# Token sums and value-bias sums bound between a tile's maximum and its reciprocal, and the block sum on VectorE, in a Hymba block on one core

## The chip, the cores and the metric

One Trainium2 chip, one of its cores. The metric is the time of one execution on the device in microseconds (us), as the median of several runs. The engines of a core work from instruction queues of their own, each strictly in its own order: TensorE (PE; matmuls, and PEld for its weight loads), VectorE (DVE), ScalarE (ACT), GpSimd (POOL) and SyncE (SP), which issues most of the transfers. Engines wait for one another by semaphores.

## What is computed

One encoder block for 512 tokens of width 2048 in float32: adaLN-modulated norm, one projection of which the columns feed 16 attention heads (64 wide, three dilated windows merged by their softmax denominators) and 4 heads of gated linear attention (GLA), gates on both, an output projection, a residual step and a last norm. Cut to what matters here:

```python
mod = jax.nn.silu(c) @ w_cond[layer] + b_cond[layer]
shift, scale, gate = jnp.split(mod, 3, axis=-1)
h = rms_norm(x) * (1.0 + scale[:, None]) + shift[:, None]
proj = h @ w_in[layer]
aq, ak, av, ag, gq, gk, gv, gg, lr_f, lr_b = jnp.split(proj, PROJ_SPLITS, axis=-1)
...
for window, dilation in DILATED_PATTERNS:
    o_p, lse_p = dilated_window_attention(aq, ak, av, rel_bias, window, dilation)
...
mix_w = jax.nn.softmax(jnp.stack(lses, axis=0), axis=0)
att = jnp.einsum('pbsh,pbshe->bshe', mix_w.astype(av.dtype), jnp.stack(outs, axis=0))
a_out = att.reshape(B, S, ATT_WIDTH) * jax.nn.silu(ag)
...
g_out = g_o * jax.nn.silu(gg)
y = jnp.concatenate([a_out, g_out], axis=-1) @ w_out[layer]
x = x + gate[:, None] * y
return rms_norm(x) * final_gain
```

## The kernel before

**Products.** Each float32 product is made of three matmuls of a reduced type (`three`, L216 to L220): high by high, low by high, high by low. The high part of a weight block (128x1024) is written by ScalarE (`split_hi`, L481), the low part by VectorE as raw minus high (`split_lo`, L466). Tiles are named by unit and block: raw_qk61 is the loaded weight, qk61h and qk61l its parts. The value projection V and the output products O save multiplications by a recursive scheme that needs sums of blocks. Sums over tokens of the normalised input (`token_sums`, from L1115; tiles S1 to S4) are made by VectorE in ten operations of 128x512 for each of four parts and stored for V. Most block sums are made in transfers that add on arrival (`paced`, L418, in GpSimd's queue). The block named T1 of the output products is the exception: two blocks are loaded (raw_O and raw_P, L380), and `whole` (L455) adds them on GpSimd, four times for each of the two pairs of output products: for O16 to O19 and O44 to O47.

**Units.** TensorE's order is the order of the program. `unit(name)` is one pass over the eight weight blocks of a projection, with side work put in at set fractions of it. The units from 190 us on are qk2, qk4, qk6, gk (each with the attention of four heads at its side), V, ag0, ag1, gg0, gg1 (each with one GLA head), and then the products O: pair 0 is O0 to O27, pair 1 is O28 to O55. On the other engines a scheduler sets the order by its estimate of when operands are there; `tc.issue_after(x)` binds one instruction behind another on its engine.

**Attention.** One tile is 128 queries of one head against 512 keys, 16 tiles a unit. VectorE adds the bias row and takes the maximum (L773, out p, st), ScalarE makes the exponential with its sum (L776), VectorE the reciprocal (L777), GpSimd the scaled probabilities p (L781), TensorE transposes p (L793), ScalarE and VectorE split the transposed tile (pt, L797 and L798), and TensorE multiplies it with the values (L807).

**Sums beside.** The shift of the norm passes through the value projection as a bias. It is a product of a row with a matrix, made by VectorE in 16 halves of 128x1024 (`bias_half`; load L882, tile rawv, sums L888 for the first and L317 for the second half of a row block). The gate of the residual step is made in the same way in 32 halves (`gate_half`, load L846, tile rawg, sums L317). Halves of one kind share the four buffers of the raw weights; the others have a pool `two` with a single buffer each for the tags l and h. Before the change the token sums and the bias sums are side work at fractions of a unit, bound behind the last low part (`last["lo"]`). `SUMS_IN` says how many bias and gate sums a unit takes, `SUM_OPS_IN` how many of the block sums by transfer.

**GLA.** In each of ag0 to gg1, `gla_head` computes a chain of states on TensorE (kv, L965) and VectorE (st, L972 and L977), masked copies of the scores (L997), the gated squares (gsq, gsl, L1027) and their sum over rows (gn).

**The last load.** One weight block of the end, O52, is loaded and split ahead of its turn; its high part is called wlast.

## Time and profile before

| | |
|---|---|
| Median of 3 runs | 943.13 us (943.1 to 943.54) |
| Profiled execution, its time | 945.4 us |
| Profiled execution, its span | 943.6 us |
| Mean granted TensorE clock | 0.989 |
| TensorE busy | 912.2 us (97%) |
| VectorE busy | 714.8 us (76%) |
| ScalarE busy | 490.6 us (52%) |
| GpSimd busy | 141.7 us (15%) |

A row of a timeline gives the start and the length in us, the engine, the line in the kernel, the operation, out<-in, the tile's shape, and in brackets the idle time before it and what ended it. A row of the waits gives who waited at which line, for what, and then total, times and longest in us. A row of the windows gives the stretch, the busy time and number of instructions of each engine (PE, PEld, DVE, ACT, POOL), the granted clock, the share of DMA time and GB/s. A row of the groups gives busy time in us and the mean of one in ns, then the idle time before them.

### The profile page before, as it was taken

To read this page: it belongs to the slowest core of one execution; us is meant where nothing else is said; L and a number is where in the kernel's file an instruction comes from. 1 tells how busy PE (TensorE), PEld (TensorE's weight loads), DVE (VectorE), ACT (ScalarE), POOL (GpSimd) and SP (SyncE) were. 2 spreads that over 40 slices of the span, in tenths; PEclk is the share of its full clock that TensorE was granted. 3 is DMA by queue.
4 is the path that set the end of the run, shared out by engine and by line. 5 is a ranking of instruction groups with operands and counts; after the bars stand their busy time and mean duration, and the time that the engine had idled before them with its cause. 6 is when DMAs were issued, how large, how long until landed. Compare 5 with 4: busy or idle time off the path is not lost.

```text
span 943.6 us, 12252 instructions
## 1 busy us (share of the span) xinstructions
PE 912.2 (97%) x4327; PEld 753.3 (80%) x4327; DVE 714.8 (76%) x1028; ACT 490.6 (52%) x790; POOL 141.7 (15%) x176
## 2 busy tenths in 40 slices
PE   8999999999999999999999999999979999999976
PEld 6888888888878788788777888888868888788854
DVE  7988899777777787787578677684957469796676
ACT  5553543555645555555567545453634157455454
POOL 0000000022223242242000112021120100400311
PEclk9999999999999999999999999999989999999989
DMA  9999497676797877986777788787866978878643
GB/s 352 404 412 376 174 371 257 217 200 195 198 266 231 258 215 217 249 234 195 226 255 248 242 250 264 223 257 255 235 194 217 289 225 317 310 237 283 234 171 141
DMA packets 62247, 238.13 MB, mean 252 GB/s; under 512 B 8197, under 2 KB 8485, under 8 KB 52841
## 3 DMA queue, kind: packets, MB, share of 16 engines
q1 hardware_dynamic: 55282, 194.77, 57.8%
q0 software_dynamic: 6464, 42.01, 19.2%
q8 instruction: 34, 0.56, 0.2%
q10 hardware_dynamic: 440, 0.57, 0.2%
q14 instruction: 27, 0.22, 0.1%
HBM read 224.64 MB, written 50.42 MB: 292 GB/s over the span
## 4 chain that ended last, share of the span: by engine, by line
PE 80%; DVE 7%; DMA 6%; ACT 3%; issue 2%; POOL 1%; SPq 0%; ACTq 0%; DVEq 0%; POOLq 0%
PE ps_qk L218 4%; PE ps_qk L220 4%; PE ps_qk L219 4%; PE g L220 3%; PE g L219 3%; PE g L218 3%; PE stb L220 3%; PE stb L218 3%; PE stb L219 3%; PE ps_ag L218 3%; PE ps_ag L220 3%; PE ps_ag L219 3%; PE o L807 3%; PE t L793 3%; PE sta L219 2%
## 5 line engine op out<-in xcount | busy, mean ns | idle before, releaser
L781 POOL TENSOR_SCALAR p<-p,st 128x512 f32<-128x512 f32 x62 | 53.7, 866 | 187.1 <-DVE st L777 164.6
L776 ACT ACTIVATE p<-p,st 128x512 f32<-128x512 f32 x64 | 46.2, 722 | 55.9 <-DVE st L773 53.9
L317 DVE CUSTOM_DVE_ANT_0 cb<-cb,sb,c_bcond 128x2048 f32<-128x2048 f32 (+1 forms) x32 | 73.5, 2296 | 1.1 <-DMA cb<-in_wm 1.1
L773 DVE CUSTOM_DVE_ANT_0 p<-s,g 128x512 f32<-128x512 f32 x64 | 43.8, 687 | 12.7 <-PE s L770 12.2
L798 DVE TENSOR_TENSOR pt<-t,pt 128x512 fp32r<-128x512 f32 x64 | 43.7, 687 | 11.9 <-ACT pt L797 11.6
L418 POOL DMA_DIRECT2D T<-in_w_o x32 | 23.2, 732 | 159.1 <-ACT V2h L481 15.3
L797 ACT ACTIVATE pt<-t 128x512 fp32r<-128x512 f32 x64 | 37.9, 591 | 14.4 <-PE t L793 13.4
L793 PEld LDWEIGHTS t<-c_ident,p 128*128 128x128 f32 x256 | 31.3, 140 | 12.4 <-POOL p L781 4.4
L793 PE MATMUL t<-c_ident,p 128*128 128x128 f32 x256 | 38.6, 273 | 2.4 <-POOL p L781 2.3
L455 POOL TENSOR_TENSOR raw_O<-raw_O,raw_P 128x1024 f32<-128x1024 f32 x8 | 21.1, 2643 | 115.3 <-DMA raw_P<-in_w_o 62.7
L807 PEld LDWEIGHTS o<-pt,vv 128*128 128x128 f32 x256 | 34.8, 188 | 2.8
L807 PE MATMUL o<-pt,vv 128*128 128x256 f32 x256 | 35.6, 281 | 0.0
L769 PE MATMUL s<-ks,qs 128*128 128x512 f32 x64 | 25.1, 392 | 1.2 <-DVE pt L798 1.2
L982 ACT ACTIVATE sq<-st,sc 128x256 f32<-128x256 f32 x24 | 12.1, 505 | 25.6 <-DVE st L972 17.6
L770 PE MATMUL s<-kl,qs 128*128 128x512 f32 x64 | 25.0, 391 | 0.0
L317 DVE CUSTOM_DVE_ANT_0 rawg<-rawg,crow,gate 128x1024 f32<-128x1024 f32 x16 | 20.4, 1280 | 5.6 <-DMA rawg<-in_wg 5.6
L418 POOL DMA_DIRECT2D T3V<-in_w_gv x8 | 5.5, 693 | 119.8 <-ACT qk21h L481 119.8
L777 DVE RECIPROCAL st<-st 128x1 f32<-128x1 f32 x64 | 10.1, 158 | 16.3 <-ACT p L776 16.3
L418 POOL DMA_DIRECT2D T<-T x16 | 9.1, 572 | 80.0 <-ACT V6h L481 13.8
L317 DVE CUSTOM_DVE_ANT_0 rawg<-rawg,crow,c_bcond 128x1024 f32<-128x1024 f32 x16 | 20.3, 1279 | 0.3 <-DMA rawg<-in_wg 0.3
L810 ACT ACTIVATE oh<-o 64x256 f32<-64x256 f32 x32 | 12.2, 382 | 12.2 <-PE o L807 11.8
L545 ACT ACTIVATE h_hi<-xt,shift 128x512 fp32r<-128x512 f32 x16 | 11.5, 718 | 13.0 <-DVE shift L317 13.0
(1640 smaller groups left out, 3081.5 us busy)
## 6 DMA issues: line engine op xcount, KB each, us to landing
cb<-in_wm SPq DMA_DIRECT2D x31, 1024.0 KB, 9.0
T<-in_w_o POOLq DMA_DIRECT2D x32, 512.0 KB, 7.2
rawg<-in_wg SPq DMA_DIRECT2D x32, 512.0 KB, 5.4
raw_O<-in_w_o SPq DMA_DIRECT2D x32, 512.0 KB, 4.3
raw_qk<-in_w_qk SPq DMA_DIRECT2D x24, 512.0 KB, 4.1
raw_O<-T SPq DMA_DIRECT2D x24, 512.0 KB, 5.3
rawb<-in_w_sb SPq DMA_DIRECT2D x16, 512.0 KB, 5.4
rawv<-in_wv SPq DMA_DIRECT2D x16, 512.0 KB, 4.7
```

What stands on the lines that cost most here:

```text
L218: mm(ps, lh, rh, start=first, stop=False, skip_group_check=more)
L219: mm(ps, ll, rh, start=False, stop=False, skip_group_check=more)
L220: mm(ps, lh, rl, start=False, stop=last, skip_group_check=more)
L317: nc.vector.tensor_tensor_reduce(out=w, in0=w, in1=with_, op0=ALU.mult, op1=ALU.add, scale=1.0, scalar=init, accum_out=dst)
L418: move = nc.gpsimd.dma_start(dst, src, max_dma_last_dim=8192, **how).ins
L773: nc.vector.tensor_tensor_reduce(out=t, in0=ps, in1=gt[h][:, P * i:P * i + 512], op0=ALU.add, op1=ALU.min, scale=1.0, scalar=3e38, accum_o ...
L776: act(t, t, AF.Exp, bias=st[:, 0:1], scale=-1.0, accum_out=st[:, 1:2])
L781: last["pool"] = nc.gpsimd.tensor_scalar(t, t, st[:, 2:3], 1.0, op0=ALU.mult, op1=ALU.mult).ins
L793: nc.tensor.transpose(pk[:, kt * P:kt * P + P], t[:, kt * P:kt * P + P], ident)
L797: act(hi, src, AF.Copy)
L798: tt(lo, src, hi.bitcast(F32), op=ALU.subtract)
L807: mm(po[:, :256], vv[h // 4][:, kt, h % 4, :], t[:, w, kt, :], start=kt == 0 and w == 0, stop=kt == 3 and w == 1)
```

## The change

A string for each attention unit, `BESIDE`, says for each of its 16 tiles whether a token operation (t), a bias sum (r) or nothing stands beside it. `beside(top)` binds that operation behind the tile's maximum, and the reciprocal is bound behind the operation. A bias sum's load is issued five tiles ahead (`BIAS_AHEAD`). The bias sums leave `SUMS_IN`; with their names gone from it, the units qk4, qk6 and gk fetch their weights three blocks ahead instead of two (L1060). gg0 takes eight gate sums instead of nine, gg1 eight instead of seven, and each gate sum's load is issued 1.1 instead of 0.8 of a sum's share ahead of the sum's number. `SUM_OPS_IN` spreads the same number of transfers a little differently. `whole` adds its two blocks on VectorE.

```diff
 GLA_AT = (0.01, 0.02, 0.33, 0.46, 0.46, 0.56, 0.64, 0.76, 0.76, 0.88)
 GLA_FIRST = (0.27, 0.32, 0.53, 0.6, 0.74, 0.78, 0.84, 0.89, 0.91, 0.97)
 
-SUMS_IN = {"qk4": 5, "qk6": 5, "gk": 6, "ag0": 8, "ag1": 8, "gg0": 9}
+SUMS_IN = {"ag0": 8, "ag1": 8, "gg0": 8}
+
+BESIDE = {"qk2": " tttt ttt ttt", "qk4": " tttttrttrtrttrr", "qk6": " rttrttrttrttrtt", "gk": "rttrttrttrttrttr"}
+BIAS_AHEAD = 5
 
 
 OUT_ORDER = ("P1", "P7", "P6", "P4", "P5", "P3", "P2")
...
 WEIGHTS = {"P1": "11", "P7": "T3", "P6": "T2", "P4": "T4", "P5": "T1", "P3": "22", "P2": "21"}
 BLOCK_SUMS = {"T3": ("12", "22"), "T2": ("T3", "11"), "T4": ("T2", "21"), "T1": ("11", "12")}
 OUT_DEEP = 6
-SUM_OPS_IN = {"qk2": 10, "qk4": 9, "qk6": 9, "gk": 8, "V": 8, "ag0": 9, "ag1": 9, "gg0": 9, "gg1": 9}
+SUM_OPS_IN = {"qk2": 10, "qk4": 10, "qk6": 10, "gk": 9, "V": 9, "ag0": 8, "ag1": 8, "gg0": 8, "gg1": 8}
 
 
 def _plan(tasks, free, ready):
...
 
     def cond_sum(dst, w, with_, init):
 
-        nc.vector.tensor_tensor_reduce(out=w, in0=w, in1=with_, op0=ALU.mult, op1=ALU.add,
-                                       scale=1.0, scalar=init, accum_out=dst)
+        return nc.vector.tensor_tensor_reduce(out=w, in0=w, in1=with_, op0=ALU.mult, op1=ALU.add,
+                                              scale=1.0, scalar=init, accum_out=dst)
 
     grow = dp.tile([NH, 1024], F32, tag="grow", name="grow")
...
     def whole(i):
         if i in second:
             t, e = raws[i], second.pop(i)
-            nc.gpsimd.tensor_tensor(t, t, e, op=ALU.add)
+            tt(t, t, e, op=ALU.add)
 
     def split(i):
         split_hi(i)
...
 
     cat = [None] * 4
 
+    side_work = []
+
+    def beside(top):
+
+        go = side_work.pop(0) if side_work else None
+        if len(side_work) >= BIAS_AHEAD and side_work[BIAS_AHEAD - 1]:
+            load = side_work[BIAS_AHEAD - 1][0]
+            if load:
+                load()
+        if not go:
+            return None
+        with tc.issue_after(top):
+            return go[1]()
+
     def attention(pairs):
 
         tiles = [(2 * p + j, i) for p in pairs for j in range(2) for i in range(4)]
...
                 mm(ps, qs[:, q], kl, start=False, stop=True)
                 t = T2(f"p{h}{i}")
                 st = sm.tile([P, 3], F32, tag="st", name=f"st{h}{i}", bufs=6)
-                nc.vector.tensor_tensor_reduce(
+                top = nc.vector.tensor_tensor_reduce(
                     out=t, in0=ps, in1=gt[h][:, P * i:P * i + 512], op0=ALU.add, op1=ALU.min,
-                    scale=1.0, scalar=3e38, accum_out=st[:, 0:1])
+                    scale=1.0, scalar=3e38, accum_out=st[:, 0:1]).ins
                 act(t, t, AF.Exp, bias=st[:, 0:1], scale=-1.0, accum_out=st[:, 1:2])
-                nc.vector.reciprocal(st[:, 2:3], st[:, 1:2])
+                held = beside(top)
+                with tc.issue_after(held) if held else nullcontext():
+                    nc.vector.reciprocal(st[:, 2:3], st[:, 1:2])
                 if (h, i) in ((15, 2), (15, 3)):
                     act(t, t, AF.Copy, scale=st[:, 2:3])
                 else:
...
 
         def go():
             raw = t[0]
-            with tc.issue_after(last["lo"]):
-                if z == 0:
-                    nc.vector.tensor_tensor_reduce(out=raw, in0=raw, in1=shb[0][:, :1024], op0=ALU.mult, op1=ALU.add,
-                                                   scale=1.0, scalar=0.0, accum_out=vbias0[:, m:m + 1])
-                else:
-                    cond_sum(vbias[:, m:m + 1], raw, shb[0][:, 1024:], vbias0[:, m:m + 1])
+            if z == 0:
+                return nc.vector.tensor_tensor_reduce(out=raw, in0=raw, in1=shb[0][:, :1024], op0=ALU.mult, op1=ALU.add,
+                                                      scale=1.0, scalar=0.0, accum_out=vbias0[:, m:m + 1]).ins
+            return cond_sum(vbias[:, m:m + 1], raw, shb[0][:, 1024:], vbias0[:, m:m + 1]).ins
         return load, go
 
-    sum_work = [bias_half(m, z) for m in range(8) for z in range(2)]
-    sum_work += [gate_half(m, z) for z in range(2) for m in range(KT)]
+    bias_work = [bias_half(m, z) for m in range(8) for z in range(2)]
+    sum_work = [gate_half(m, z) for z in range(2) for m in range(KT)]
 
     def some_sums(name):
         r = [sum_work.pop(0) for _ in range(SUMS_IN.get(name, len(sum_work)))]
         n = len(r)
-        loads = [(max(q - 0.8, 0.05) / n, x[0]) for q, x in enumerate(r)]
+        loads = [(max(q - 1.1, 0.05) / n, x[0]) for q, x in enumerate(r)]
         return sorted(loads + [((q + 0.7) / n, x[1]) for q, x in enumerate(r)], key=lambda x: x[0])
 
     def gla_head(h):
...
 
         def sub(n, h, th, kh):
             made[n], made[n + "3"] = pair_tile(f"{n}{kp}")
-            tt(made[n + "3"], h_part(h, th, kh, kp), h_part(h, 1, 0, kp), op=ALU.subtract)
+            return tt(made[n + "3"], h_part(h, th, kh, kp), h_part(h, 1, 0, kp), op=ALU.subtract).ins
 
         def low_sub(n, th, kh):
-            sub(n + "e", h_lo, th, kh)
+            return sub(n + "e", h_lo, th, kh)
 
         def whole_sum(n):
-            tt(made[n], made[n], made[n + "e"], op=ALU.add)
+            i = tt(made[n], made[n], made[n + "e"], op=ALU.add).ins
             s_store(n, kp, made[n])
+            return i
 
         def s2():
             made["S2"], made["S23"] = pair_tile(f"S2{kp}")
-            stt(made["S23"], made["S13"], -1.0, h_part(h_hi, 0, 0, kp), op0=ALU.mult, op1=ALU.subtract)
+            return stt(made["S23"], made["S13"], -1.0, h_part(h_hi, 0, 0, kp), op0=ALU.mult, op1=ALU.subtract).ins
 
         def s2_low():
-            tt(made["S23"], made["S23"], h_part(h_lo, 0, 0, kp), op=ALU.subtract)
+            i = tt(made["S23"], made["S23"], h_part(h_lo, 0, 0, kp), op=ALU.subtract).ins
             s_store("S2", kp, made["S2"])
+            return i
 
         def s4():
             made["S4"], made["S43"] = pair_tile(f"S4{kp}")
-            tt(made["S43"], made["S23"], h_part(h_hi, 0, 1, kp), op=ALU.add)
+            return tt(made["S43"], made["S23"], h_part(h_hi, 0, 1, kp), op=ALU.add).ins
 
         def s4_low():
-            tt(made["S43"], made["S43"], h_part(h_lo, 0, 1, kp), op=ALU.add)
+            i = tt(made["S43"], made["S43"], h_part(h_lo, 0, 1, kp), op=ALU.add).ins
             s_store("S4", kp, made["S4"])
+            return i
 
         parts = [lambda: sub("S3", h_hi, 0, 0), lambda: low_sub("S3", 0, 0), lambda: whole_sum("S3"),
                  lambda: sub("S1", h_hi, 1, 1), lambda: low_sub("S1", 1, 1), lambda: whole_sum("S1"),
                  s2, s2_low, s4, s4_low]
 
-        def held(go):
-            def run():
-                with tc.issue_after(last["lo"]):
-                    go()
-            return run
-        return [((q + 0.3) / len(parts), held(go)) for q, go in enumerate(parts)]
+        return parts
 
     cond_row = dp.tile([1, 2048], F32, tag="cond_row", name="cond_row")
     nc.sync.dma_start(cond_row, sb[0:1, :])
...
 
     for p in range(2):
         qk_evict(p, psb["b", 4 + 2 * p], psb["b", 5 + 2 * p])
+    for kp, n in enumerate(("qk2", "qk4", "qk6", "gk")):
+        sums = token_sums(kp)
+        for c in BESIDE[n].ljust(16):
+            side_work.append(None if c == " " else (None, sums.pop(0)) if c == "t" else bias_work.pop(0))
+        assert not sums
+    assert not bias_work
+
     for n, p in (("qk2", 0), ("qk4", 2), ("qk6", 4)):
-        ps = unit(n, False, attention((p, p + 1)) + token_sums(p // 2)
-                  + ([(0.05, shift_row)] if p == 2 else []) + (some_sums(n) if p else []))
+        ps = unit(n, False, attention((p, p + 1)) + ([(0.05, shift_row)] if p == 2 else []))
         for q in range(2):
             qk_evict(p + 2 + q, ps[2 * q], ps[2 * q + 1])
 
-    ps = unit("gk", False, attention((6, 7)) + token_sums(3) + some_sums("gk"))
+    ps = unit("gk", False, attention((6, 7)))
     gla["k"] = B8("gkt", [4, 512])
     for i in range(4):
         act(gla["k"][:, i, :], ps[i], AF.Copy)
```

TensorE's order is the same in both. The rows below give line, operation, out<-in and shape; the changed kernel's lines are 3 to 21 higher. On VectorE, in the middle of unit qk4 (names: p and st of head 7, tile 0 and 1; pt, t the transposed tile; qk60l a low part), before:

```order
L773 ISA p70_2688,st70_2689<-s70_2685,g7_2584 128x512
L773 ISA st70_2689 128x1
L777 RECIPROCAL st70_2689<-st70_2689 128x1
L798 TENSOR_TENSOR pt61_2700<-t62_2701,pt61_2700 128x4x128
L466 TENSOR_TENSOR qk60l_2816<-raw_qk60_2731,qk60h_2815 128x1024
L773 ISA p71_2739,st71_2740<-s71_2736,g7_2584 128x512
L773 ISA st71_2740 128x1
L814 TENSOR_TENSOR cat0_1594<-o60_2716,oh60_2725 64x256
L888 ISA rawv20_2654,vbias0_1495<-rawv20_2654,shb_2263 128x1024
```

and in the changed kernel (head 6, tiles 1 and 2; rawv01 is a bias sum, S21 a token sum):

```order
L790 ISA p61_2590,st61_2591<-s61_2587,g6_2433 128x512
L790 ISA st61_2591 128x1
L320 ISA rawv01_2393,vbias_1494<-rawv01_2393,shb_2259,vbias0_1495 128x1024
L320 ISA vbias_1494 128x1
L796 RECIPROCAL st61_2591<-st61_2591 128x1
L817 TENSOR_TENSOR pt51_2558<-t53_2605,pt51_2558 128x4x128
L790 ISA p62_2618,st62_2619<-s62_2615,g6_2433 128x512
L790 ISA st62_2619 128x1
L1151 TENSOR_TENSOR S21_2542<-S21_2542,h_lo_154 128x512
```

The sums stand between a maximum (ISA p, st) and its reciprocal, one for a tile.

On VectorE in the unit gg0, where the gate sums (rawg) meet the chain of states (st300 and what follows), before:

```order
L317 ISA rawg41_6140,gate_1492<-rawg41_6140,crow1_5771,gate0_1493 128x1024
L317 ISA gate_1492 128x1
L317 ISA rawg51_6197,gate_1492<-rawg51_6197,crow1_5771,gate0_1493 128x1024
L317 ISA gate_1492 128x1
L972 TENSOR_SCALAR st300_6182<-kv300_6177,sc30_6007 128x256
L1336 TENSOR_TENSOR A11l_6431<-cat0_1594,A11h_6430 128x1024
L1336 TENSOR_TENSOR A11l_6431<-cat1_2986,A11h_6430 128x1024
L977 SCALAR_TENSOR_TENSOR st301_6186<-kv300_6177,sc30_6007,dc301_6187 128x256
```

and in the changed kernel:

```order
L989 TENSOR_SCALAR st300_6184<-kv300_6179,sc30_6012 128x256
L1357 TENSOR_TENSOR A11l_6429<-cat1_2984,A11h_6428 128x1024
L994 SCALAR_TENSOR_TENSOR st301_6188<-kv300_6179,sc30_6012,dc301_6189 128x256
L469 TENSOR_TENSOR gg06l_6264<-raw_gg06_6211,gg06h_6263 128x1024
L994 SCALAR_TENSOR_TENSOR st302_6193<-kv301_6180,sc30_6012,dc302_6194 128x256
L989 TENSOR_SCALAR st310_6231<-kv310_6226,sc31_6039 128x256
L994 SCALAR_TENSOR_TENSOR st311_6235<-kv310_6226,sc31_6039,dc311_6236 128x256
L994 SCALAR_TENSOR_TENSOR st312_6240<-kv311_6227,sc31_6039,dc312_6241 128x256
L469 TENSOR_TENSOR gg07l_6312<-raw_gg07_6266,gg07h_6311 128x1024
L1014 COPY_PREDICATED at3_6281<-c_maskf_1486,att30_6271 128x512
L1016 SCALAR_TENSOR_TENSOR at3_6281<-c_ident_1484,at3_6281 128x512
L320 ISA rawg51_6206,gate_1492<-rawg51_6206,crow1_5762,gate0_1493 128x1024
```

The sum of rawg51 has moved from ahead of st300 to behind the whole chain and the masked copy of at3.

On VectorE in pair 1 of the output products, from the low part O40l on (x, y and gx belong to the residual step of the pair before), before:

```order
L466 TENSOR_TENSOR O40l_7608<-raw_O40_7524,O40h_7607 128x1024
L466 TENSOR_TENSOR O41l_7632<-raw_O41_7546,O41h_7631 128x1024
L466 TENSOR_TENSOR O42l_7652<-raw_O42_7570,O42h_7651 128x1024
L466 TENSOR_TENSOR O43l_7672<-raw_O43_7588,O43h_7671 128x1024
L466 TENSOR_TENSOR O44l_7693<-raw_O44_7610,O44h_7692 128x1024
L466 TENSOR_TENSOR O45l_7724<-raw_O45_7634,O45h_7723 128x1024
L1430 TENSOR_TENSOR y23_7711<-gx10_7465,u210_7627 128x512
L1430 TENSOR_TENSOR y33_7717<-gx11_7466,u211_7629 128x512
L1423 TENSOR_TENSOR y23_7711<-y23_7711,gate_b_6749 128x512
L1423 TENSOR_TENSOR y33_7717<-y33_7717,gate_b_6749 128x512
L1424 TENSOR_TENSOR x11_7551<-y23_7711,x11_7551 128x512
L1424 TENSOR_TENSOR x11_7551<-y33_7717,x11_7551 128x512
```

and in the changed kernel:

```order
L469 TENSOR_TENSOR O40l_7608<-raw_O40_7524,O40h_7607 128x1024
L458 TENSOR_TENSOR raw_O44_7610<-raw_O44_7610,raw_P44_7612 128x1024
L469 TENSOR_TENSOR O41l_7632<-raw_O41_7546,O41h_7631 128x1024
L469 TENSOR_TENSOR O42l_7652<-raw_O42_7570,O42h_7651 128x1024
L458 TENSOR_TENSOR raw_O45_7634<-raw_O45_7634,raw_P45_7636 128x1024
L458 TENSOR_TENSOR raw_O46_7654<-raw_O46_7654,raw_P46_7656 128x1024
L469 TENSOR_TENSOR O43l_7672<-raw_O43_7588,O43h_7671 128x1024
L469 TENSOR_TENSOR O44l_7693<-raw_O44_7610,O44h_7692 128x1024
L458 TENSOR_TENSOR raw_O47_7674<-raw_O47_7674,raw_P47_7676 128x1024
L1451 TENSOR_TENSOR y23_7711<-gx10_7465,u210_7627 128x512
L469 TENSOR_TENSOR O45l_7724<-raw_O45_7634,O45h_7723 128x1024
```

The four additions of raw_P, which were the last work in GpSimd's order ahead of the last norm, now stand among the low parts, that of O47 ahead of O45l.

## The prediction

> **What bounds the kernel now.** I read the page first (span and busy shares), then TensorE's waits, then the windows, because a share of 97% says nothing about where the other 3% lie.
>
> ```profile
> span 943.6 us, 12252 instructions
> PE 912.2 (97%) x4327; PEld 753.3 (80%) x4327; DVE 714.8 (76%) x1028; ACT 490.6 (52%) x790; POOL 141.7 (15%) x176
> ...
> PE kv L965 <- DVE st L977: 5.3, 1, 5.3
> PE g L218 <- ACT O47h L481: 2.9, 1, 2.9
> ...
> PE t L793 <- POOL p L781: 2.3, 3, 0.9
> PE g L220 <- DVE O46l L466: 2.0, 1, 2.0
> ...
> PE g L220 <- DVE O18l L466: 1.0, 1, 1.0
> ```
>
> TensorE is the bound. Its instructions stand in the same order in both kernels, so the change can only take away or add time in which TensorE waits, and time at a lowered clock. A wait's columns are total, times, longest. The windows place them (TensorE, weight load, VectorE, ScalarE, GpSimd busy, then the granted clock, the DMA share and GB/s):
>
> ```profile
> 200.00:260.00 60.00, 59.37 (x323) 49.76 (x322) 44.04 (x91) 35.97 (x72) 17.23 (x26) 1.00 0.71 198
> 260.00:330.00 70.00, 67.61 (x357) 56.31 (x356) 53.22 (x110) 37.27 (x72) 19.40 (x25) 1.00 0.85 252
> 330.00:400.00 70.00, 68.87 (x364) 57.52 (x363) 54.67 (x111) 38.93 (x74) 21.53 (x25) 1.00 0.81 228
> ...
> 550.00:680.00 130.00, 130.00 (x639) 109.75 (x638) 95.88 (x131) 68.02 (x109) 18.77 (x31) 1.00 0.80 252
> 690.00:700.00 10.00, 4.69 (x18) 3.55 (x17) 6.04 (x8) 2.91 (x4) 4.21 (x3) 0.87 0.53 179
> 700.00:710.00 10.00, 10.00 (x45) 8.32 (x44) 4.41 (x8) 3.46 (x6) 1.75 (x3) 0.79 0.54 125
> 810.00:830.00 20.00, 19.04 (x84) 15.47 (x83) 18.77 (x18) 10.17 (x16) 6.56 (x3) 1.00 0.94 345
> 890.00:900.00 10.00, 8.43 (x38) 6.64 (x36) 9.37 (x9) 1.80 (x2) 4.91 (x2) 1.00 0.63 214
> 900.00:910.00 10.00, 5.64 (x16) 3.79 (x17) 6.04 (x11) 5.12 (x8) 0.00 (x0) 0.78 0.50 176
> 910.00:920.00 10.00, 10.00 (x41) 8.15 (x40) 8.60 (x11) 7.33 (x13) 1.15 (x1) 0.88 0.48 173
> ```
>
> Four places lose time within reach of the change. **A**, the unit gg0 at 690 to 710: 5.31 us idle, and 10 × 0.13 + 10 × 0.21 = 3.4 us at the lowered clock, 8.7 together. **B**, the second pair of output products at 890 to 920: 1.57 + 4.36 idle and 10 × 0.22 + 10 × 0.12 = 3.4 of clock, 9.3 together. **C**, the first pair: 0.96. **D**, the attention units: 0.63 + 2.39 + 1.13 = 4.15. The clock falls only behind the two long stops; the shorter stops of C and D leave it at 1.00.
>
> The Trainium skill, page "TensorE: Matmul & The Clock Gate", section "What's actually happening", says that the clock halves after an idle window of about 3.4 us; the trace agrees, as the windows around the 5.3 us stop show and those around stops of 1 us do not. By that rule a stop that shrinks from 5.3 to 2 us gives back the clock's 3.4 us too; read from the rows alone, A and B pay the clock together with the stop.
>
> **Part A, the gate sums.** What VectorE did there:
>
> ```profile
> 693.28 1.28 DVE L317 CUSTOM_DVE_ANT_0 rawg<-rawg,crow,gate 128x1024 f32<-128x1024 f32 x1 [5.58 <-DMA rawg<-in_wg]
> ...
> 719.49 0.68 DVE L1027 TENSOR_TENSOR gsl<-gsq,gsh 128x512 fp32r<-128x512 f32 x1
> ```
>
> A gate sum waited 5.58 us for its transfer and stood ahead of the state st300, on which the chain to kv (5.3 us) hangs. gg0 had nine sums; it now has eight, as ag0 and ag1 have, and in the new order this sum stands behind the whole state chain and the masked copies. The nearest rows for that placement are those of ag0 and ag1: 130.00 of 130.00 us busy from 550 to 680. Between no loss (those windows) and the full 8.7 I take 0.3 left, since the placement is the same and the sums' loads are issued 0.3 of a sum earlier. So A gives **−8.4**. What is late next: a sum that waits now holds the splits behind it and, at the end of gg0, the chain to gsl, which ended at 719.49 + 0.68. That is rival 2.
>
> **Part B, the block sums.** Eight sums of two loaded 128x1024 blocks move from GpSimd to VectorE.
>
> ```profile
> 880.24 3.10 POOL L455 TENSOR_TENSOR raw_O<-raw_O,raw_P 128x1024 f32<-128x1024 f32 x1 [61.20 <-DMA raw_P<-in_w_o]
> 886.67 5.73 POOL L455 TENSOR_TENSOR raw_O<-raw_O,raw_P 128x1024 f32<-128x1024 f32 x2 [3.33 <-DVE O43l L466]
> 896.23 2.51 POOL L455 TENSOR_TENSOR raw_O<-raw_O,raw_P 128x1024 f32<-128x1024 f32 x1 [3.82 <-DMA raw_O<-in_w_o]
> ...
> 902.67 1.06 ACT L481 ACTIVATE wlast<-raw_O 128x1024 fp32r<-128x1024 f32 x1 [9.17 <-DMA raw_O<-in_w_o]
> ...
> 904.86 1.04 ACT L481 ACTIVATE O47h<-raw_O 128x1024 fp32r<-128x1024 f32 x1
> ...
> 890.77 2.71 DVE L466 TENSOR_TENSOR O45l<-raw_O,O45h 128x1024 fp32r<-128x1024 f32 x1 [0.63 <-ACT O45h L481]
> ...
> 895.55 0.39 PE L220 MATMUL g<-O45l,c_h 128*128 128x512 f32 x1
> ...
> L1232 DVE TENSOR_TENSOR vS<-rawS,vS 128x1024 fp32r<-128x1024 f32 x8 | 9.7, 1221 | 1.5 <-ACT vS L1231 1.5
> ```
>
> This is one chain: each sum frees the buffer that the next load needs. It holds four sums (3.10 + 5.73 + 2.51 = 11.34) and three gaps with a load (3.33, 3.82, and from 898.74 to 902.67 3.93). ScalarE works in order, so O47h stood behind wlast, which waited 9.17 us for the last of these loads; TensorE's 2.9 us for O47h comes from there. VectorE adds two 128x1024 blocks in 1.22 (the vS row, the same operation and shape with another output type), so four sums take 4.88 and the chain is 6.46 shorter: wlast at 896.2, O47h 2.19 behind it at 898.4, done by 899.4. Without stops TensorE comes to O47 at 895.55 + 22 × 0.227 = 900.5 (0.227 from the starts of successive matmuls, 895.55 and 895.78). So that wait is gone with 1.1 to spare.
>
> What VectorE pays is 4 × 1.22 = 4.9 us in a stretch in which it was 9.37 of 10 busy; but that busy time holds splits that were stretched beside GpSimd's sums (O45l 2.71 instead of about 1.22), so most of it is given back. Queued behind a waiting sum are the splits of the blocks before it: sum47 stands ahead of O45l, which TensorE needs at 895.55. By the chain above sum47 starts at 896.23 − 1.88 − 2 × 1.64 = 891.1 at the earliest (1.88 and 1.64: what the first and each of the next two sums save), O45l ends near 894 to 895. O46l, behind four additions of y and x, comes at about 898.5 against its need at 898.3. I take 1.0 of loss left, between 0 and 3 (one transfer gap). B gives **−8.3**.
>
> The Trainium skill, page "SBUF — State Buffer", section "Who interferes with whom", says that a VectorE instruction with two SBUF inputs and a GpSimd instruction that reads SBUF exclude each other for a whole instruction. The O45l row agrees: 2.71 beside a GpSimd sum. By that rule the splits fall back to the 1.22 used above; the same rule speaks against the attention part, since the bound sums would hold up GpSimd's normalisation of probabilities.
>
> **Part C, the same sums in the first pair.**
>
> ```profile
> 813.36 3.33 DVE L466 TENSOR_TENSOR O17l<-raw_O,O17h 128x1024 fp32r<-128x1024 f32 x1 [0.52 <-ACT O17h L481]
> ...
> 820.71 1.22 DVE L466 TENSOR_TENSOR O18l<-raw_O,O18h 128x1024 fp32r<-128x1024 f32 x1
> ...
> raw_O<-in_w_o SPq DMA_DIRECT2D x32, 512.0 KB, 4.3
> ```
>
> O17l loses its 2.1 us of stretch, but O16l and O17l now stand behind sums 17 to 19, and the load for sum 19 waits for a buffer that an earlier split frees behind sum 17. With 4.3 us for that load O17l ends between 819 and 820 and O18l between 823 and 824; the old stop here was 0.96. The new loss lies between 0 and 3; I take 2, so C costs **+1.0**.
>
> **Part D, the bound sums beside attention.** 40 token operations and 16 bias sums exist before and after; nothing is added, they move to between a tile's maximum and its reciprocal.
>
> ```profile
> 270.48 1.23 DVE L888 CUSTOM_DVE_ANT_0 rawv<-rawv,shb 128x1024 f32<-128x1024 f32 x1 [2.17 <-DMA shb<-srow]
> ...
> 315.57 1.22 DVE L466 TENSOR_TENSOR qk61l<-raw_qk,qk61h 128x1024 fp32r<-128x1024 f32 x1
> 316.71 0.16 DVE L777 RECIPROCAL st<-st 128x1 f32<-128x1 f32 x1
> 316.78 1.27 DVE L317 CUSTOM_DVE_ANT_0 rawv<-rawv,shb,vbias 128x1024 f32<-128x1024 f32 x1
> ...
> 312.61 0.69 POOL L781 TENSOR_SCALAR p<-p,st 128x512 f32<-128x512 f32 x1 [2.09 <-DVE st L777]
> ...
> 317.04 1.57 POOL L781 TENSOR_SCALAR p<-p,st 128x512 f32<-128x512 f32 x1 [3.01 <-DVE st L777]
> ...
> 316.46 0.60 PE L793 MATMUL t<-c_ident,p 128*128 128x128 f32 x4
> ```
>
> Between maximum and reciprocal VectorE waits for ScalarE's exponential anyway, so a bias sum (1.27) sets a reciprocal back by less than its length. For a middle tile that is covered: its p ends at 312.61 + 0.69 = 313.30 and is transposed at 316.46, 3.16 us later. Without this cover each of the 16 would cost up to 1.27. The last tile of a unit has no such cover: there TensorE goes straight from p to the transposes, and the three waits of 2.3 us are of that kind (317.04 + 1.57 = 318.61). At the end of qk4 the reciprocal now stands ahead of qk61l but behind a bias sum of about the same length: no change there. What goes: the wait of the first bias sum for its row (2.17, which made a stop of about 1.3), now ordered seven tiles into qk4; the first tile of qk4, which had two token operations ahead of its maximum and now has one behind it (0.63 in the window 200 to 260); and some of the rest. Of 4.15, 2.1 go: **−2.1**, between 0 and −3.
>
> The weights of qk4, qk6 and gk are fetched three instead of two ahead, and each bias sum holds its buffer for five tiles. At the start of V, the second block's buffer is freed by the last bias sum:
>
> ```profile
> 450.49 0.69 DVE L773 CUSTOM_DVE_ANT_0 p<-s,g 128x512 f32<-128x512 f32 x1 [0.89 <-PE s L770]
> ...
> 462.41 0.39 PE L220 MATMUL ps_gv_P<-V1l,h_hi 128*128 128x512 f32 x1
> ...
> rawv<-in_wv SPq DMA_DIRECT2D x16, 512.0 KB, 4.7
> ```
>
> Last maximum to 451.2, sum to 452.4, load 4.7, splits 1.04 + 1.22: 459.4, needed at 462.41. 3 us of cover that a queue on SP can eat; I take **+0.3**, and **+0.5** for places that I could not follow (GpSimd's queue gives up 8 sums and takes DMA issues in another rhythm).
>
> **Sum:** −8.4 − 8.3 + 1.0 − 2.1 + 0.3 + 0.5 = −17.0. The profiled span of 943.6 becomes 926.6. The run of that profile took 945.4, 2.3 over the median 943.13, so the sum is applied to the median: **926.1**.
>
> **The rivals.** *One: sums that wait for transfers hold the splits behind them.* VectorE works in order, GpSimd had nothing behind its sums. If sum47 and sum19 each wait one transfer gap (3.3 to 3.9) longer than I assume, B keeps a stop of about 3 with its 3.4 of clock and C loses 3: 926.1 + 5.4 + 1 = **932.5**. For it: VectorE already waited 5.58 for a transfer in A. Against: both loads are issued as soon as a buffer is free, and buffers now come free 6.46 sooner.
>
> *Two: the stop of A only moves.* The sums stay bound in VectorE's order; the late one now stands ahead of a split and of the last sums of gg0, and the load after it needs its buffer. If the chain to gsl is 2 to 4 late, a stop of 3 with 3.4 of clock replaces A: 926.1 + 6.1 = **932.2**. For it: gsl needs the end of this very queue. Against: the 130.00 of 130.00 in the two units with eight sums.
>
> *Three, the other side: the bound bias sums wait.* A sum in front of a reciprocal whose transfer is late holds that tile's p, the next pt and the next maximum. It decides once a wait exceeds the cover of 3.16; with 16 sums it takes about 17 / 16 + 3.16 = 4.2 us of wait for each to eat the whole gain. At half of them waiting 6.5, the loss is 8 × 3.3 = 27: **953**. For it: odd halves share one buffer, so a load can wait for an earlier sum. Against: five tiles are 5 × 260 / 64 = 20 us (64 tiles between 200 and 460), and the transfer takes 4.7.
>
> *Four: the binding does nothing.* The sums fall where they fell and D stays: 926.1 + 2.1 = **928.2**. For it: the first maxima's stops may come from the matmuls ahead of them, not from the sums.
>
> **How the numbers follow.** Forecast 0.60, own range 919 to 931 (A from 0 to 2 left, B and C from 0 to 3 each, D from 0 to −3, V from 0 to 2); rival one 0.12; two 0.12; three 0.10; four 0.06. The range 919 to 936 leaves out rival three, a gain beyond 24, and rivals one and two with both losses at once: not quite 2 in 10. This kernel's measurement cannot tell 0.2% (1.9 us) from nothing. Rival three is slower in 0.09 of its 0.10, and 0.01 lies within; one and two together may add 0.01 there; the rest is faster: 0.89.
>
> **What would show it.** A: TensorE busy over 9.8 of 10 in the windows of the old stop, granted clock 1.00, no wait of kv on st over 0.5. B: four VectorE sums of about 1.2 us, wlast before 898, no wait for O47h, clock 1.00 at its place. C: a wait for O17l or O18l of 0 to 3. D: GpSimd's p waiting for st as before, only the waits at the ends of units left. I am wrong if TensorE waits for p in middle tiles, if a clock under 1.00 stays in either place, or if VectorE shows waits on bias transfers above 3 us.

## The result, and the profile after

| | Before | After |
|---|---|---|
| Median on one chip | 943.34 us (943.1 to 944.27, 4 runs) | 928.09 us (926.28 to 931.5, 4 runs) |
| Ratio | | 0.9841, 95% interval 0.9812 to 0.987 |
| Profiled execution: time, span | 945.4, 943.6 us | 931.5, 929.7 us |

The kernel became 15.3 us faster; 17.0 were forecast, and 928.09 stands in the range of 919 to 936. Both profiled executions lie above their medians: the changed kernel's by 3.4 us, as the slowest of its four, and the one before by 2.1.

First TensorE's waits in the changed kernel (its lines are 3 to 21 higher than before), those of 0.5 us and more, without sta and warm at the kernel's start:

```profile
PE ps_gv_P L221 <- DVE gv L1318: 2.2, 1, 2.2
PE g L223 <- DVE O55l L469: 1.9, 1, 1.9
PE t L812 <- POOL p L800: 1.5, 2, 0.8
...
PE g L223 <- DVE O18l L469: 0.8, 1, 0.8
PE g L223 <- DVE O46l L469: 0.5, 1, 0.5
```

The waits of kv (5.3) and of O47h (2.9) are gone. Two rows were not among the prediction's: gv in V, and O55l, the low part of the last block. The windows say what each costs with its clock. First one row of the kernel before that was not shown yet, the unit V:

```profile
460.00:550.00 90.00, 88.59 (x417) 71.00 (x416) 60.70 (x67) 52.20 (x75) 7.19 (x12) 1.00 0.77 244
```

and then the changed kernel:

```profile
200.00:260.00 60.00, 59.98 (x326) 50.50 (x325) 44.16 (x90) 35.12 (x68) 16.65 (x26) 1.00 0.75 199
260.00:330.00 70.00, 68.86 (x364) 57.66 (x363) 53.02 (x109) 38.38 (x73) 18.04 (x26) 1.00 0.88 254
330.00:400.00 70.00, 69.38 (x367) 58.38 (x367) 55.70 (x115) 38.26 (x74) 17.44 (x27) 1.00 0.83 239
...
460.00:550.00 90.00, 87.64 (x409) 71.02 (x408) 57.26 (x62) 49.85 (x71) 6.87 (x12) 0.98 0.78 250
690.00:700.00 10.00, 10.00 (x54) 8.63 (x53) 6.40 (x9) 3.92 (x7) 3.48 (x5) 1.00 0.65 177
700.00:710.00 10.00, 10.00 (x66) 9.03 (x65) 7.33 (x11) 2.89 (x4) 0.78 (x1) 1.00 0.88 243
800.00:820.00 20.00, 19.23 (x85) 15.53 (x84) 18.71 (x22) 10.30 (x16) 0.00 (x0) 1.00 0.88 315
880.00:890.00 10.00, 9.47 (x42) 7.28 (x41) 7.64 (x11) 4.11 (x6) 0.00 (x0) 1.00 0.75 261
890.00:900.00 10.00, 10.00 (x46) 8.21 (x45) 9.96 (x17) 6.81 (x12) 0.00 (x0) 1.00 0.47 159
900.00:910.00 10.00, 9.84 (x44) 7.83 (x42) 9.55 (x13) 7.05 (x13) 2.72 (x2) 1.00 0.56 210
910.00:920.00 10.00, 8.21 (x28) 6.33 (x28) 5.95 (x13) 3.90 (x10) 1.25 (x1) 0.83 0.09 35
```

| Place | Lost before | Lost after | Change | Forecast |
|---|---|---|---|---|
| A, gg0 | 8.7 | 0.0 | −8.7 | −8.4 |
| B, second output pair | 9.3 | 0.5 | −8.8 | −8.3 |
| C, first output pair | 1.0 | 0.8 | −0.2 | +1.0 |
| D, attention | 4.15 | 0.02 + 1.14 + 0.62 = 1.8 | −2.4 | −2.1 |
| V | 1.4 | 2.36 + 90 × 0.02 = 4.2 | +2.8 | +0.3 |
| O55l, at the end | 0 | 0.16 + 1.79 + 10 × 0.17 = 3.7 | +3.7 | 0 |
| Not followed | | | | +0.5 |

The column adds to −13.6, against −13.9 in the spans. In the table, "lost" is idle time plus time at the lowered clock. A second reading needs neither: TensorE's order is the same in both kernels and both traces hold its 4327 matmuls, so the starts of the same matmul can be compared. By them A gives −8.5, B −8.2, C −0.2, D −3.1, V +1.8 and O55l +3.8, −14.4 up to the last matmul (934.06 before, 919.63 after); from there to the end the changed kernel took 0.5 longer. So V cost 1 us less than the table says and D gave 0.7 more; the rest agrees.

VectorE's timeline shows how B was won:

```profile
869.88 1.23 DVE L458 TENSOR_TENSOR raw_O<-raw_O,raw_P 128x1024 f32<-128x1024 f32 x1 [1.56 <-DMA raw_P<-in_w_o]
...
875.55 1.22 DVE L458 TENSOR_TENSOR raw_O<-raw_O,raw_P 128x1024 f32<-128x1024 f32 x1 [1.80 <-DMA raw_O<-in_w_o]
877.00 1.23 DVE L458 TENSOR_TENSOR raw_O<-raw_O,raw_P 128x1024 f32<-128x1024 f32 x1 [0.23 <-DMA raw_P<-in_w_o]
...
882.58 1.23 DVE L458 TENSOR_TENSOR raw_O<-raw_O,raw_P 128x1024 f32<-128x1024 f32 x1 [2.08 <-DMA raw_O<-in_w_o]
...
884.32 1.22 DVE L469 TENSOR_TENSOR O45l<-raw_O,O45h 128x1024 fp32r<-128x1024 f32 x1
```

and ScalarE's what became of wlast:

```profile
887.65 1.06 ACT L484 ACTIVATE wlast<-raw_O 128x1024 fp32r<-128x1024 f32 x1 [4.28 <-DMA raw_O<-in_w_o]
...
889.23 1.04 ACT L484 ACTIVATE O47h<-raw_O 128x1024 fp32r<-128x1024 f32 x1
```

Four sums of 1.23 us in place of 11.34 in all, O45l at 1.22 instead of 2.71, and wlast waits 4.28 instead of 9.17. From the first sum to wlast there are now 17.8 us (887.65 − 869.88), before 22.4 (902.67 − 880.24); the gaps between, each with a load, went from 3.3, 3.8 and 3.9 to 4.4, 4.3 and 3.8.

### The profile page after: what moved, and what is told of

It is laid out like the page before. It is cut to its first block, busy times and chain, and to the rows that moved or that the text cites. A ratio compares the mean times of both kernels' runs of the same rounds, so it can differ in the third digit from the quotient of the medians.

```text
span 929.7 us, 12256 instructions
## 1 busy us (share of the span) xinstructions
PE 908.2 (98%) x4327; PEld 752.8 (81%) x4327; DVE 712.9 (77%) x1036; ACT 490.0 (53%) x790; POOL 109.8 (12%) x168
## 4 chain that ended last, share of the span: by engine, by line
PE 83%; DVE 7%; DMA 4%; issue 3%; ACT 3%; POOL 0%; SPq 0%; DVEq 0%; ACTq 0%; POOLq 0%
PE ps_qk L221 4%; PE ps_qk L223 4%; PE ps_qk L222 4%; PE o L826 3%; PE stb L223 3%; PE stb L221 3%; PE stb L222 3%; PE ps_ag L221 3%; PE ps_ag L222 3%; PE ps_ag L223 3%; PE t L812 3%; PE g L223 3%; PE sta L222 2%; PE g L222 2%; PE g L221 2%
## 5 line engine op out<-in xcount | busy, mean ns | idle before, releaser
L800 POOL TENSOR_SCALAR p<-p,st 128x512 f32<-128x512 f32 x62 | 43.7, 705 | 191.3 <-DVE st L796 146.6
L816 ACT ACTIVATE pt<-t 128x512 fp32r<-128x512 f32 x64 | 37.8, 591 | 11.5 <-PE t L812 10.8
L1478 POOL TENSOR_SCALAR x<-x,rn 128x512 f32<-128x512 f32 x3 | 4.0, 1324 | 161.8 <-ACT rn L1467 159.2
L833 DVE TENSOR_TENSOR cat<-o,oh 64x256 f32<-64x256 f32 x32 | 13.3, 416 | 7.7 <-ACT oh L829 7.2
L548 ACT ACTIVATE h_hi<-xt,shift 128x512 fp32r<-128x512 f32 x16 | 11.5, 719 | 12.9 <-DVE shift L320 12.9
```

The costliest lines, as they stand in the source:

```text
L800: last["pool"] = nc.gpsimd.tensor_scalar(t, t, st[:, 2:3], 1.0, op0=ALU.mult, op1=ALU.mult).ins
L816: act(hi, src, AF.Copy)
```

## The experiments

Each run has its own median and a ratio to the kernel before, run beside it on the same chip; runs of one group share a chip. One kernel's runs spread over 2 to 9 us, so single stops are read in the profiles, and the medians are used for what is above 2 us.

**One part alone.** Four kernels on one chip (before: 942.08 us, 26 runs from 936.95 to 945.96).

The block sums alone (e1_sum_on_vector):

```diff
-            nc.gpsimd.tensor_tensor(t, t, e, op=ALU.add)
+            tt(t, t, e, op=ALU.add)
```

> The kernel before with only the eight block sums on VectorE. Theory (three separate gains, and a new stop at O55l that the moved sums bring, because with them VectorE's order has O55l behind six operations on x and y): the stop in the second output pair falls from 9.3 to about 0.7, a stop at O55l of about 2 us with 1.6 us at the lowered clock appears, the 8.7 us at gg0 stay: 943.3 - 8.6 + 3.7 = 938.4 us (937 to 940). Rival (the O55l stop has nothing to do with the sums): no stop there, 934.7 us. Rival (the sums on VectorE give nothing alone): 942 to 945.

Measured: 938.01 us, ratio 0.9958 (0.9933 to 0.9983), −4.1 on this chip where the theory had −4.9 from 943.3. Neither rival came. The stop at O55l is there with the sums alone, but shorter than expected and at the full clock, so the nearness to the theory's 938.4 is in part luck:

```profile
PE kv L965 <- DVE st L977: 5.3, 1, 5.3
...
PE g L220 <- DVE O55l L466: 1.4, 1, 1.4
PE g L220 <- DVE O18l L466: 1.1, 1, 1.1
...
PE g L220 <- DVE O46l L466: 0.4, 1, 0.4
```

The gate sums alone (e2_gate_eight):

```diff
-SUMS_IN = {"qk4": 5, "qk6": 5, "gk": 6, "ag0": 8, "ag1": 8, "gg0": 9}
+SUMS_IN = {"qk4": 5, "qk6": 5, "gk": 6, "ag0": 8, "ag1": 8, "gg0": 8}
```

> The kernel before with eight instead of nine gate sums in gg0 and nothing else. Theory (the place of one gate sum behind the chain of states is all of the gain at gg0): no stop and a full clock from 690 to 710, 943.3 - 8.7 = 934.6 us (933.5 to 936). Rival (the earlier loads of the changed kernel are needed too): a stop of 2 to 5 us stays, 937 to 942.

Measured: 935.88 us, ratio 0.9941 (0.9919 to 0.9963), −6.2 on this chip (interval −7.6 to −3.5) where −8.7 was expected; the kernel before had a median of 942.08 here and ran from 936.95 on, while the 8.7 were read in an execution of 945.4. The wait of kv is gone from the profile altogether, and by the starts of the same matmuls this run gains the same 8.5 us at that place as the whole change. So one number in a table is all of A; the earlier loads are not needed for it. The stops of B remain in this run, in smaller pieces:

```profile
PE g L220 <- DVE O46l L466: 2.1, 1, 2.1
PE g L220 <- DVE O47l L466: 1.5, 1, 1.5
...
PE g L218 <- ACT O47h L481: 0.7, 1, 0.7
```

The binding alone (e3_bound_only), the changed kernel with its other parts undone:

```diff
-SUMS_IN = {"ag0": 8, "ag1": 8, "gg0": 8}
+SUMS_IN = {"ag0": 8, "ag1": 8, "gg0": 9}
...
-SUM_OPS_IN = {"qk2": 10, "qk4": 10, "qk6": 10, "gk": 9, "V": 9, "ag0": 8, "ag1": 8, "gg0": 8, "gg1": 8}
+SUM_OPS_IN = {"qk2": 10, "qk4": 9, "qk6": 9, "gk": 8, "V": 8, "ag0": 9, "ag1": 9, "gg0": 9, "gg1": 9}
...
-            tt(t, t, e, op=ALU.add)
+            nc.gpsimd.tensor_tensor(t, t, e, op=ALU.add)
...
-        loads = [(max(q - 1.1, 0.05) / n, x[0]) for q, x in enumerate(r)]
+        loads = [(max(q - 0.8, 0.05) / n, x[0]) for q, x in enumerate(r)]
```

> The changed kernel with the block sums back on GpSimd, nine gate sums in gg0, their loads at 0.8 and the old spread of the added transfers: what is left is the binding of token and bias sums between maximum and reciprocal, and the weights fetched one block further ahead. Theory: only the stops beside attention go, -2.4: 941 us (940 to 942.5), no stop at O55l. Rival (the binding carries most of the gain): under 936. Rival (the stop of V16 is longer because of the binding): 943 to 944, with a stop of over 2 us in V.

Measured: 940.62 us, ratio 0.9988 (0.9968 to 1.0008). The median lies where the theory had it, but the interval reaches from 3.0 us faster to 0.8 slower and so takes in no change: the median alone does not show that the binding does anything. Its profile does: the windows of D lose 0.02, 1.15 and 0.62 as in the changed kernel, and there are two waits of p instead of three. The wait of kv (5.4) is there, O55l is not.

The changed kernel with only the block sums back on GpSimd (e4_sum_on_gpsimd), the first diff reversed:

> The changed kernel with only the block sums back on GpSimd. Theory: the 9.3 us in the second output pair return, the stop at O55l goes: 928.1 + 8.6 - 3.7 = 933 us (931.5 to 935). Rival (O55l's stop is independent of the sums): 936.7 us.

Measured: 932.79 us, ratio 0.9911 (0.9878 to 0.9944): the theory's 933. O47h waits 2.3 us again, and O55l does not stop. It shows gv in V at 2.2, as the changed kernel does and e3 (0.7) does not.

**The two new stops.** Four kernels on another chip (before: 943.21 us, 7 runs). The changed kernel itself (e5_again):

> The changed kernel as it is, beside the next three on the same chip. 928 us (926 to 930), with stops at V16 (2.2 us) and at O55l (1.9 us).

Measured: 927.8 us (925.58 to 931.46), ratio 0.9838 (0.9807 to 0.9869). Its profiled execution had a span of 923.9, gv at 0.4 instead of 2.2, no stop at O18l, and O55l at 2.0. So gv and O18l differ between executions of one kernel; O55l does not.

The old spread of the added transfers (e6_old_spread), the second of the four pieces of e3's diff alone:

> The changed kernel with the spread of the added transfers over the units as it was before (eight instead of nine in V, nine instead of eight in ag0 to gg1). Theory (the longer stop of V16 comes from the ninth transfer in V, beside which the load of V17 took 7.5 us): the stop of V16 falls from 2.4 to the 1.3 to 1.5 of the kernel before, 1 to 2.5 us faster than the changed kernel on the same chip. Rival (it comes from the bound bias sums, which hold a buffer at the start of V): the stop stays at 2.2 and the time within 0.7 us.

Measured: 928.26 us, ratio 0.9844 (0.9827 to 0.986): no gain in the median. gv is at 0.7. Over all profiles, the seven others with the old spread (before, e1, e2, e3, e8, e10, e11) have 0.7 too, the six with the new spread 2.2, 2.2, 0.4, 2.2, 2.0 and 2.1. The spread sets this stop in most executions, but the median does not show it. The profiles show where it went. A stop that falls from 2.1 (the changed kernel again, e12 below) to 0.7 is worth only 0.9 us by the starts of the same matmuls around it, as long as the clock stays at 1.00, which it did in both. In e6 0.6 of that was lost again in the first 60 us, which differ by 1.0 us among the three profiles of the changed kernel itself.

The residual operations of the last but one product behind O55l (e7_low_part_first):

```diff
-        for n in range(2):
-            add_up(n, r, summed(g2[n], v[n], ALU.subtract), True)
+        def rows_of_r(r=r, g2=g2, v=v):
+            for n in range(2):
+                with tc.issue_after(last["lo"]):
+                    add_up(n, r, summed(g2[n], v[n], ALU.subtract), True)
+        if end:
+            todo.setdefault((1, "P2", 3), []).append(rows_of_r)
+        else:
+            rows_of_r()
...
-        s = [first_squares(n, [0, 1, r]) for n in range(2)]
         product(pair, "P2", g3, True, True, (0,))
+        s = [first_squares(n, [0, 1, r]) for n in range(2)]
```

> The changed kernel with the residual operations of the last but one product bound behind the low part O55l, so that O55l stands next to O54l in VectorE's order. Theory (O55l stops TensorE only because six operations on x and y stand ahead of it): no wait for O55l, full clock to the end, 2.1 + 1.6 = 3.7 us faster than the changed kernel. Rival (the six operations then hold up the last norm): 0 to 1 us faster.

Measured: 928.4 us (924.31 to 929.6), ratio 0.9833 (0.9806 to 0.9859). O55l is gone from the waits, but the time is that of e5; of the two expectations the rival's is the nearer. With e6's spread as well (e8_both):

> Both edits together. Theory: the two gains add, 4.7 to 6 us faster than the changed kernel on the same chip, about 922.5 us. Rival (the old spread has no effect): 3.7 us faster.

Measured: 926.79 us, ratio 0.9821 (0.9804 to 0.9837): 1.5 us under e6 and 1.0 under e5; neither the 4.7 to 6 of the theory nor the rival's 3.7 came. What happened is read behind TensorE's end, in VectorE's timeline of e8 (TensorE's last matmul starts at 912.97):

```profile
911.92 0.68 DVE L1445 TENSOR_TENSOR x<-y,x 128x512 f32<-128x512 f32 x1
913.96 0.75 DVE L1476 SCALAR_TENSOR_TENSOR x<-x,rn,fgain 128x512 f32<-128x512 f32 x1 [1.35 <-ACT rn L1467]
914.63 0.68 DVE L1451 TENSOR_TENSOR y<-g,p 128x512 f32<-128x512 f32 x1
```

The last row's y (L1451) came behind the norm of the row before, which waited 1.35 for ScalarE; in e6 the same y waits for TensorE instead. That is the mechanism of e7's rival. From the start of the last matmul to the end, the changed kernel takes 10.1 us in each of its three profiles, and so does e6, but e7 takes 11.5 and e8 11.3. So some 1.2 us of the 2.0 us stop come back behind TensorE's end. The 1.6 us of clock, which the theory of e7 counted too, were not there to be won in e5 and e6: behind their stops the clock stayed at 1.00.

**The tail, the unit ends and the load's lead.** Four kernels on a third chip (before: 942.32 us, 13 runs). The changed kernel again (e12_again), the measure of this group:

> The changed kernel once more on the chip of e9 to e11, as their measure: 926 to 930 us, with the stop at O55l.

Measured: 927.7 us (927.14 to 930.85), ratio 0.9854 (0.9822 to 0.9886).

Only the second row behind O55l, with the old spread (e10_second_row_behind); against e7 the first row's call stays where it was:

```diff
-        def rows_of_r(r=r, g2=g2, v=v):
-            for n in range(2):
-                with tc.issue_after(last["lo"]):
-                    add_up(n, r, summed(g2[n], v[n], ALU.subtract), True)
+        def row(n, r=r, g2=g2, v=v):
+            add_up(n, r, summed(g2[n], v[n], ALU.subtract), True)
+
+        def second_row():
+            with tc.issue_after(last["lo"]):
+                row(1)
+        row(0)
         if end:
-            todo.setdefault((1, "P2", 3), []).append(rows_of_r)
+            todo.setdefault((1, "P2", 3), []).append(second_row)
         else:
-            rows_of_r()
+            row(1)
```

> The changed kernel with the old spread of the added transfers and with only the second row's three residual operations bound behind O55l; with both rows behind it (the run e8) the stop went, but the last norm began 1.3 us after TensorE's end. Theory: a stop of 0.3 to 0.5 us at O55l, no fall of the clock, TensorE's end followed by the last norm at once: 3 us faster than the run e6, about 925 us. Rival (the stop stays over 1 us because the first row's operations alone hold O55l): 927 to 928 us.

Measured: 927.25 us, ratio 0.9847 (0.9816 to 0.9879). The stop is 0.2 us, better than the theory had it, and still the median is 0.45 from e12's, so the 925 expected did not come. Its profile has 0.5 us at O45l, which e12 has not, and the last row's y is still behind the norm of the row before (915.68 behind 915.01). By the starts of the same matmuls the stretch with O55l is 1.6 us shorter than in e12, of which 0.8 come back behind TensorE's end and 0.5 are lost around O45l. What is left of the stop at O55l stays below what these medians can tell.

The empty place of qk4 and qk6 in the last tile (e11_last_tile_free), on top of e10:

```diff
-BESIDE = {"qk2": " tttt ttt ttt", "qk4": " tttttrttrtrttrr", "qk6": " rttrttrttrttrtt", "gk": "rttrttrttrttrttr"}
+BESIDE = {"qk2": " tttt ttt ttt", "qk4": "tttttrttrtrttrr ", "qk6": "rttrttrttrttrtt ", "gk": "rttrttrttrttrttr"}
```

> The kernel of e10 with the empty place of qk4 and of qk6 moved from the first to the last tile. Theory (in the last tile the low part stood right behind the reciprocal, and GpSimd's p, which took 1.51 us instead of 0.69, could not start beside that VectorE operation with two inputs in SBUF; without a sum there, the low part goes ahead of the reciprocal and p is alone): p of the last tile 0.7 us, the two stops of 1.0 and 0.8 us at the ends of qk4 and qk6 fall to 0.3 or less, 1.3 to 1.8 us faster than e10. Rival (these stops come from the chain of exponential, reciprocal and p, whatever stands beside it): the stops stay at 0.8 to 1.0.

Measured: 924.76 us (922.76 to 926.08), ratio 0.9809 (0.9774 to 0.9844), 2.5 us under e10 and 2.9 under the changed kernel on this chip; the ratios' intervals overlap. In the profile the theory is plain at the end of qk4. GpSimd in the last tile there, in the changed kernel:

```profile
314.81 1.51 POOL L800 TENSOR_SCALAR p<-p,st 128x512 f32<-128x512 f32 x1 [3.21 <-DVE st L796]
```

VectorE beside it:

```profile
314.48 0.16 DVE L796 RECIPROCAL st<-st 128x1 f32<-128x1 f32 x1
314.56 1.21 DVE L469 TENSOR_TENSOR qk61l<-raw_qk,qk61h 128x1024 fp32r<-128x1024 f32 x1
```

and GpSimd in e11, where qk61l goes first, with the windows of both unit ends:

```profile
314.15 0.69 POOL L800 TENSOR_SCALAR p<-p,st 128x512 f32<-128x512 f32 x1 [3.19 <-DVE st L796]
...
260.00:330.00 70.00, 69.98 (x370) 58.88 (x369) 54.90 (x112) 39.12 (x74) 19.28 (x25) 1.00 0.84 249
330.00:400.00 70.00, 69.98 (x371) 58.85 (x371) 55.76 (x117) 39.16 (x77) 18.69 (x28) 1.00 0.82 236
```

TensorE loses 0.04 us in 140, where it lost 1.76. At the end of qk4 the reciprocal starts 1.1 us behind the read-out of its maximum in both kernels (313.33 and 314.48, in e11 312.68 and 313.82), so there the length of p alone made the stop of 0.85. At the end of qk6 it was the other way: p was alone and as short before the edit, and the stop of 0.62 came from the chain, as the rival had it. There a token operation and the low part gk1l stood between the maximum (read out at 381.04) and its reciprocal, in the changed kernel:

```profile
382.78 0.16 DVE L796 RECIPROCAL st<-st 128x1 f32<-128x1 f32 x1
383.11 0.69 POOL L800 TENSOR_SCALAR p<-p,st 128x512 f32<-128x512 f32 x1 [4.03 <-DVE st L796]
```

and in e11 gk1l alone (the maximum was read out at 379.01):

```profile
380.15 0.15 DVE L796 RECIPROCAL st<-st 128x1 f32<-128x1 f32 x1
380.48 0.69 POOL L800 TENSOR_SCALAR p<-p,st 128x512 f32<-128x512 f32 x1 [3.35 <-DVE st L796]
```

By its median this kernel is the fastest of all that ran. The Trainium skill, page "SBUF — State Buffer", section "Who interferes with whom", says that a VectorE instruction with two inputs in SBUF and a GpSimd instruction that reads SBUF shut each other out for a whole instruction; the pair of 1.51 and 0.69 agrees.

Each bias sum's load one tile ahead instead of five (e9_load_one_tile_ahead):

```diff
-BIAS_AHEAD = 5
+BIAS_AHEAD = 1
```

> The changed kernel with each bias sum's load issued one tile (about 4 us) ahead instead of five. It puts a price on the rival of the prediction in which bound sums wait for their transfers: a transfer takes 4.7 us, so a sum should come 1 to 3 us late and hold the reciprocal behind it. Theory (a middle tile's cover of 3.2 us takes this up): VectorE shows waits on rawv of 10 to 40 us in all, yet the time stays within 3 us of the changed kernel. Rival (the waits go through to TensorE): 16 times 1 to 3 us, 944 to 970 us.

Measured: 936.81 us, ratio 0.9939 (0.9918 to 0.9959), 9.1 over e12. Neither theory foresaw how: the waits of 10 to 40 us did not come, and the time lies between the two. The groups of VectorE show that no sum waited to speak of: the idle time before both is 0.0.

```profile
L320 DVE CUSTOM_DVE_ANT_0 rawv<-rawv,shb,vbias 128x1024 f32<-128x1024 f32 x8 | 10.2, 1279 | 0.0
L906 DVE CUSTOM_DVE_ANT_0 rawv<-rawv,shb 128x1024 f32<-128x1024 f32 x8 | 10.0, 1245 | 0.0
```

One of them came late all the same, the last, and VectorE's order has four other operations between V1l and it. Its load stands behind V1's, which takes the same single buffer first; SyncE issued it at 448.90, when V1l (447.65, 1.22 long) had freed that:

```profile
448.90 0.33 SPq L901 DMA_DIRECT2D rawv<-in_wv  x1
```

VectorE and TensorE from there:

```profile
453.87 1.28 DVE L320 CUSTOM_DVE_ANT_0 rawv<-rawv,shb,vbias 128x1024 f32<-128x1024 f32 x1
...
455.08 0.16 DVE L796 RECIPROCAL st<-st 128x1 f32<-128x1 f32 x1
...
456.93 0.48 PE L812 MATMUL t<-c_ident,p 128*128 128x128 f32 x1 [7.08 <-ACT p L798]
...
450.00:457.00 7.00, 0.07 (x1) 0.08 (x2) 4.51 (x7) 3.51 (x5) 0.00 (x0) 0.76 0.56 185
457.00:461.00 4.00, 4.00 (x15) 3.42 (x16) 1.21 (x2) 1.19 (x2) 0.00 (x0) 0.57 0.77 236
```

The maximum of that tile was done at 447.7, its reciprocal at 455.2, held by the sum in between. One bound sum that is late in a tile without cover cost 6.9 us of idle time and 4 × 0.43 = 1.7 of clock behind it, 8.6 in all. This is rival three of the prediction, at one place of its sixteen; the other operations that the order put ahead of the sum filled the time in which it would have waited.

## Why the prediction was right, point by point

- **Forecast 926.1, measured 928.09; −17.0 against −15.3.** The two large terms were right in mechanism and, in the profiles, in size: A −8.4 against −8.7 (−8.5 by equal matmuls), B −8.3 against −8.8 (−8.2). e2 and e4 show each by itself, and e3 shows that the binding does neither. In medians A is less sure: e2 gives −6.2, and its interval ends at −7.6. That the total came within 2 us is in part luck. Losses at two places were not foreseen, V and O55l; D gave 1.0 more than forecast by equal matmuls and C cost 1.2 less. And the losses were read in an execution 2.1 us over the median that they were taken from.
- **A.** Eight sums, as ag0 and ag1 have, were the whole of it. The sum of rawg51 waited no more, because it now starts at 699.04 behind the masked copies. Rival two (the stop only moves) did not come.
- **B.** The chain was the cause: wlast waits 4.28 for its load, and the wait for O47h is gone. The chain became 4.6 us shorter, not 6.46, because the gaps with the loads grew; that was enough.
- **C.** I took +1.0 for sums that hold O17l and O18l. It came out at −0.2 in one execution and at no stop at all in e5. O17l takes no 3.33 us any more and does not appear among the waits there. But e7, e9 and e11, which have the same sums at that place, show 0.5 to 0.6 at O17l and 0.9 to 1.1 at O18l. So the place differs between executions by more than the term, and +1.0 was too much for some and about right for others.
- **D.** −2.1 forecast, −2.4 measured (−3.1 by equal matmuls). I wrote that at the end of qk4 nothing changes because a bias sum takes qk61l's place before the reciprocal. The stop did stay, 0.90 before and 0.85 after, but the chain was not what made it. Before, the bias sum followed the reciprocal and p took 1.57 us beside it; now qk61l follows and p takes 1.51. e11 shows that this was the stop there, and that at the end of qk6 it was the chain.
- **The clock.** I wrote that a stop that shrinks to 2 us gives the clock back. That failed in the profiled execution: the stops of 2.2 and 1.9 us that came new were each followed by 4 us at about 0.6, by the windows 3.5 of the 6.5 us that the next point tells of. In e5 and e12, the same kernel, the clock stayed at 1.00 behind such stops.
- **V and the end: +0.3 and nothing forecast, +2.8 and +3.7 found in the profiled execution** (+1.8 and +3.8 by equal matmuls; in e12, where the clock holds, +0.1 and +2.1). These two are the missing part, terms that the sum put at almost nothing. For V I looked at its first block and at what the bias sums hold there. The stop is at the 17th block: gv stands behind the low part V17l in VectorE's order, and V17h waited 4.31 us for its load. It goes with the ninth added transfer in V, which I had not priced at all. For O55l I read the order around O44 to O47 only. The moved sums changed the order 30 rows further on, and e1 and e4 show that they did it.
- **Rival one** (VectorE's sums hold the splits) is in the row of O46l with 0.5 us and, in the executions named under C, in those of O17l and O18l; nothing like its 6 us came. **Rival three** did not happen with five tiles of lead; e9 shows that it is real with one tile of lead and costs 9 us for one sum. **Rival four** (the binding does nothing) is not excluded by e3's interval, though the windows of D show 2.4 us, in e3 as in the changed kernel.

## What to carry to other kernels

A stop of 5 us costs its clock too, and one of 2 us may, so look first for the one instruction in an in-order queue that waits for a transfer and stands ahead of a chain; moving that one was worth more than the 56 operations that were bound with care. Moving work to another engine changes the scheduler's order well away from the moved instructions: compare the whole order, to the end, not only the places where the work was. Where VectorE and GpSimd take turns on one tile, put VectorE's two-input operation ahead of the hand-over, not behind it, as long as the chain has room for it: at the end of qk6 it had not.
